# Index scores of a sparse-attention branch: plain float32 products replaced by one-pass products of split operands

## The chip, the cores and the metric

The kernel runs on one core of a Trainium2 chip. The metric is the time of one execution on the device in microseconds; the median of several runs is used. The core's engines work side by side, each with its own instruction queue: TensorE (matrix products; PE in the profile, with its weight loads as PEld), VectorE (DVE), ScalarE (ACT), GpSimd (POOL) and the DMA queues, most of which SyncE (SP) feeds.

## The reference

The model is a trunk of two layers on 256 tokens with 2048 channels. Each layer normalises its input, multiplies it by one large matrix and splits the result among three token mixers: a sparse attention, a convolution and a stick-breaking attention. Their gated outputs are merged and projected, and added to the input. The change touches the indexer of the sparse attention, which chooses for every query the 64 keys that it may attend to:

```python
qi = apply_rope(qi.reshape(b, s, IDX_HEADS, IDX_DIM), cos, sin)      # 16 heads of 128
ki = apply_rope(ki.reshape(b, s, 1, IDX_DIM), cos, sin)[:, :, 0]     # one key head
wi = wi * (IDX_HEADS ** -0.5) * (IDX_DIM ** -0.5)
...
for start in range(0, s, BLOCK_Q):                                   # blocks of 128 queries
    end = start + BLOCK_Q
    rel = jnp.einsum('bthd,bsd->bhts', qi[:, start:end], ki[:, :end])
    score = jnp.einsum('bhts,bth->bts', jax.nn.relu(rel), wi[:, start:end])
    score = jnp.where(causal[None], score, NEG_INF)
    _, idx = lax.top_k(score, min(top_k, end))                       # top_k = 64
    valid = idx <= tq[None, :, None]
    ...
```

So a score is a sum over 16 heads of a weight times the positive part of a product of a query and a key. The first 64 queries have at most 64 keys before them, so all of these are chosen and no score is needed.

## The kernel before

All large products go through `unit` (its parts in lines 238 to 277) and `mult` (line 280). A unit is 512 KB of a weight matrix: SyncE loads it into one of six buffers `raw` (line 253), ScalarE casts it to a rounded type, the high part `wh` (line 264), and VectorE subtracts that from the original, which leaves the low part `wl` (line 269). `wh` and `wl` have three buffers each. The activations are kept in high and low parts too, and a float32 product becomes three one-pass products: high by high, high by low and low by high. They add up in PSUM. A plain float32 product, without parts, is one call that TensorE runs as several passes.

`chunk_W`, `chunk_N` and `chunk_T` run over the units of one stretch of columns. `chunk_T` leaves the result transposed, channels on partitions. At the end of each unit `background` lets one waiting piece of smaller work put its instructions in: the steps of a `turn_in` (a transposition by DMA, lines 172 to 188) or of one of the first two `stages`, which are generators that say after how many units they want to go on. VectorE, ScalarE and the queues follow an order that is laid out by a scheduler from program order, with `high_priority` for casts, subtractions and the evacuation of results.

Around the change a layer runs in this order. The four stick-breaking stages are started; then come the chunks for the index key (`O_KI`), values and index weights, keys, and attention queries (`O_QA`, two chunks, each turned in and rotated by `spin`, lines 794 to 798, some time later). `finish` ends the stages. Then 8 chunks give the index queries, two heads each, for the tokens from 64 on (192 of 256). Each is evacuated by `summed` (lines 305 and 306) into a small buffer `ev` (three of them) and rotated by `rope` (lines 404 to 409), which writes into the tile `qiT`. The first 64 tokens of `qiT` are filled with zeros by GpSimd. A flag holds the convolution's work back during these chunks.

After that, `index(0)` and `index(1)` are started as stages and run beside the chunks of the merge gates. For each block of 128 queries, four groups of four heads are multiplied in plain float32 (line 820), ScalarE takes the positive part (line 823), and VectorE adds each head, times its weight, to the scores (line 826). Then VectorE chooses: eight rounds of the eight largest (line 831) and their replacement (line 832), and a mask from what was replaced (lines 833 and 834).

Of the kernel before, what the change touches and what calls it, by code (L numbers as in the profile page):

```python
# [54 lines left out]
def trunk(ctx: ExitStack, tc: tile.TileContext, x, xt, w_in, w_a, w_b, w_c, w_out,  # L55
# [37 lines left out]
    def nm(s):  # L93
        uid[0] += 1
        return f"{s}_{uid[0]}"
# [4 lines left out]
    def big():  # L100
        return [slot(), slot()]

    def at(b, k):
        return b[k // KC][:, k % KC, :]
# [92 lines left out]
    def start(gen):  # L197
        stages.append([gen, 0])
# [197 lines left out]
    def pair(n):  # L396
        return tuple(tp.tile([P, n], F32R, tag=t, bufs=2, name=nm(t)) for t in ("ph", "pl"))

    def rope(acc, dst):
        a, a3 = summed(acc)  # L400
        nh, nt = a3.shape[1:]
        sw = ev()[:, :nh * nt]
        with tc.high_priority():
            nc.scalar.copy(sw[0:64, :], a[64:128, :])
            nc.scalar.copy(sw[64:128, :], a[0:64, :])
            s3 = sw.rearrange("p (h t) -> p h t", h=nh)
            nc.vector.tensor_mul(dst, a3, cos2[:, :nh, S - nt:])
            nc.vector.tensor_mul(s3, s3, sin2[:, :nh, S - nt:])
            nc.vector.tensor_add(dst, dst, s3)

    def sigmoid_of(a):
        sg = ev()
        with tc.high_priority():
            nc.scalar.activation(sg, a, AF.Sigmoid)
        return sg.rearrange("p (h t) -> p h t", h=2)

    def gate(c0, o, b, w, hx, park=None, slots=True, turn=TURN):
        def gated(k, z, v):
# [71 lines left out]
    for layer in range(DEPTH):  # L490
# [281 lines left out]
            start(stick(h0))  # L772

        hold[0] = True
        kk_ = t4()
        kaT = kk_[:, :2 * S].rearrange("p (c t) -> p c t", c=2)
        kiT = kk_[:, 2 * S:3 * S].rearrange("p (c t) -> p c t", c=1)
# [5 lines left out]
        for t in range(NT):  # L783
            with tc.high_priority():
                split(va[0][:, t, :], va[1][:, t, :], a[t][:, :256])
                nc.scalar.mul(wi[:, t, :], a[t][:, 256:256 + NIH], WI_SCALE)
        rope(chunk_T(w, O_KA, 256, hx, KD), kaT)

        qaT = slot()
# [8 lines left out]
                nc.vector.tensor_add(a3, a3, s3)  # L798
# [12 lines left out]
        def index(t, qiT=qiT, kiT=kiT, wi=wi, bias=bias):  # L811
            n = (t + 1) * P
            cb = cst[:, C_CB + S - n:C_CB + S]
            sc = tp.tile([P, S], F32, tag="sc", bufs=2, name=nm("sc"))
            bs = tp.tile([P, S], F32, tag="bias", bufs=2, name=nm("bias"))
            for g in range(NIH // 4):
                ps = mm_tile()
                for q in range(4):
                    hd = g * 4 + q
                    nc.tensor.matmul(ps[:, q * n:(q + 1) * n], at(qiT, hd)[:, t * P:(t + 1) * P],  # L820
                                     kiT[:, 0, :n], start=True, stop=True)
                rl = t4()
                nc.scalar.activation(rl[:, :4 * n], ps[:, :4 * n], AF.Relu)
                for q in range(4):
                    hd = g * 4 + q
                    nc.vector.scalar_tensor_tensor(sc[:, :n], rl[:, q * n:(q + 1) * n], wi[:, t, hd:hd + 1],
                                                   cb if hd == 0 else sc[:, :n], op0=ALU.mult, op1=ALU.add)
                yield 2
            for _ in range(TOPK // 8):
                m8 = small(8)  # L830
                nc.vector.max(m8, sc[:, :n])
                nc.vector.match_replace(sc[:, :n], m8, sc[:, :n], TAKEN)
            nc.vector.tensor_scalar(bs[:, :n], sc[:, :n], -2e38, NEG, op0=ALU.is_gt, op1=ALU.mult)
            nc.vector.tensor_tensor(bs[:, :n], bs[:, :n], cb, op=ALU.min)
            bias[t] = bs
# [417 lines left out]
```

## Time and profile before

| what | value |
| --- | --- |
| median of 3 runs | 2019.34 us (2019.0 to 2019.47) |
| span of the profiled execution | 2016.9 us |
| TensorE busy | 2005.8 us, 9550 matmuls |
| VectorE busy | 1577.9 us |
| ScalarE busy | 1388.3 us |
| GpSimd busy | 104.8 us |
| bytes moved by DMA | 458.66 MB, mean 227 GB/s |
| granted TensorE clock | 0.999 |
| plain index products, first block (64 records) | 8.4 us busy |
| plain index products, second block (64 records) | 15.1 us busy |
| query chunks of layer one | 312.5 to 386.8 us |

The span goes from the first to the last instruction of one profiled execution; the median counts some 2.4 us around it. Busy time counts an engine as busy from the start of an instruction to its end, and matmuls overlap, so their durations are longer than the distance of their starts. An arrow such as "<-DVE wl L269" names what ended a wait: here VectorE's write of `wl` in line 269.

### The profile page before, as it was taken

The numbers are of one execution on the slowest core, as the hardware profiler recorded it, in microseconds if no ns is written. First come the engines' busy times: TensorE is split into PE (matmuls) and PEld (weight loads), VectorE is DVE, ScalarE is ACT, GpSimd is POOL, SyncE is SP. The second block draws the span as 40 slices with busy tenths as digits, with TensorE's granted clock in tenths as the row PEclk, the third lists the DMA queues.
The fourth block names the chain that finished last, engine by engine and source line by source line (L and its number), as shares of the span: only waits on it lengthen the run. The fifth ranks groups of instructions, "written<-read, shape, count | busy, mean of one in ns | idle before, by whom it ended". The sixth has DMA issues, their size and how long they took to land.

```text
span 2016.9 us, 26722 instructions
## 1 busy us (share of the span) xinstructions
PE 2005.8 (99%) x9550; PEld 1699.3 (84%) x9550; DVE 1577.9 (78%) x1750; ACT 1388.3 (69%) x1952; POOL 104.8 (5%) x160
## 2 busy tenths in 40 slices
PE   9999999999999999999999999999999999999998
PEld 7888889988888888888888888899888888888887
DVE  8688767897798888866676887678967988788665
ACT  7899666687776555556658986676877765555653
POOL 0000000000001200110000000000000012002100
PEclk9999999999999999999999999999999999999999
DMA  8787666656988877889867775676678789768983
GB/s 285 215 227 213 179 178 204 214 178 195 253 237 261 272 245 236 262 267 263 267 198 216 217 211 175 177 205 209 188 206 255 227 261 302 219 230 273 283 268 126
DMA packets 340278, 458.66 MB, mean 227 GB/s; under 512 B 109104, under 2 KB 159024, under 8 KB 340016
## 3 DMA queue, kind: packets, MB, share of 16 engines
q1 hardware_dynamic: 327040, 420.88, 69.7%
q0 software_dynamic: 11648, 33.56, 5.1%
q10 hardware_dynamic: 1456, 2.51, 0.4%
q8 instruction: 75, 1.23, 0.2%
q14 instruction: 59, 0.48, 0.1%
HBM read 413.37 MB, written 20.97 MB: 215 GB/s over the span
## 4 chain that ended last, share of the span: by engine, by line
PE 98%; DMA 1%; DVE 0%; ACT 0%; issue 0%; ACTq 0%; SPq 0%; DVEq 0%
PE acc L280 87%; PE mm L280 8%; PE mm L820 1%; PE mm L857 1%; PE mm L895 0%; PE mm L764 0%; PE mm L728 0%; DMA s<-s 0%; DMA raw<-in_w_in_dram 0%; DVE wl L269 0%; PE mm L750 0%; PE mm L731 0%; PE mm L766 0%; PE mm L755 0%; PE mm L752 0%
## 5 line engine op out<-in xcount | busy, mean ns | idle before, releaser
L280 PE MATMUL acc<-wh,s 128*128 128x512 f32 (+2 forms) x4736 | 1157.0, 386 | 1.2 <-ACT wh L264 1.1
L269 DVE TENSOR_TENSOR wl<-raw,wh 128x1024 fp32r<-128x1024 f32 (+2 forms) x714 | 857.2, 1207 | 294.8 <-ACT wh L264 277.0
L280 PEld LDWEIGHTS acc<-wh,s 128*128 128x128 f32 x4736 | 875.6, 188 | 177.4 <-ACT wh L264 1.5
L264 ACT CAST wh<-raw 128x1024 fp32r<-128x1024 f32 (+2 forms) x713 | 738.8, 1039 | 387.3 <-PE acc L280 304.5
L280 PE MATMUL acc<-wl,s 128*128 128x512 f32 (+2 forms) x2368 | 622.6, 385 | 0.0
L280 PEld LDWEIGHTS acc<-wl,s 128*128 128x128 f32 x2368 | 439.5, 188 | 89.1 <-DVE wl L269 0.2
L442 ACT ACTIVATE t<-s,cst 128x255 f32<-128x255 f32 (+14 forms) x480 | 199.9, 487 | 0.0
L445 DVE TENSOR_TENSOR s<-s,t 128x1020 f32<-128x1020 f32 (+14 forms) x120 | 138.4, 1153 | 0.0
L280 PE MATMUL acc<-s,wh 128*128 128x384 f32 (+1 forms) x608 | 125.8, 348 | 0.0
L280 PE MATMUL mm<-wh,s 128*128 128x512 f32 x448 | 119.7, 389 | 0.0
L280 PEld LDWEIGHTS acc<-s,wh 128*128 128x128 f32 x608 | 104.2, 189 | 3.2
L280 PEld LDWEIGHTS mm<-wh,s 128*128 128x128 f32 x448 | 84.1, 188 | 17.4
L231 POOL COPY sm<-sm 128x3 f32<-128x3 f32 x64 | 52.6, 821 | 544.6 <-ACT sm L230 544.6
L280 PEld LDWEIGHTS acc<-s,wl 128*128 128x128 f32 x608 | 79.0, 191 | 1.9 <-DVE wl L269 0.9
L280 PE MATMUL acc<-s,wl 128*128 128x192 f32 (+1 forms) x608 | 79.5, 273 | 0.6 <-DVE wl L269 0.6
L264 ACT CAST wh<-s 128x1024 fp32r<-128x1024 f32 x32 | 33.6, 1049 | 66.1 <-DVE s L1046 58.6
L280 PE MATMUL mm<-wl,s 128*128 128x512 f32 x224 | 69.1, 390 | 0.0
L264 ACT CAST wh<-t 128x1024 fp32r<-128x1024 f32 x32 | 33.6, 1050 | 40.5 <-DVE t L1046 28.0
L269 DVE TENSOR_TENSOR wl<-s,wh 128x1024 fp32r<-128x1024 f32 x32 | 39.2, 1225 | 24.0 <-ACT wh L264 23.7
L280 PEld LDWEIGHTS mm<-wl,s 128*128 128x128 f32 x224 | 41.9, 188 | 9.0 <-DVE wl L269 0.4
L269 DVE TENSOR_TENSOR wl<-t,wh 128x1024 fp32r<-128x1024 f32 x32 | 39.1, 1222 | 9.9 <-ACT wh L264 7.1
L1046 DVE TENSOR_TENSOR t<-raw,raw 128x1024 f32<-128x1024 f32 x32 | 39.0, 1219 | 0.0
(220 smaller groups left out, 1260.6 us busy)
## 6 DMA issues: line engine op xcount, KB each, us to landing
raw<-in_w_in_dram SPq DMA_DIRECT2D x570, 512.0 KB, 4.4
raw<-in_w_out_dram SPq DMA_DIRECT2D x64, 512.0 KB, 5.1
raw<-in_w_b_dram SPq DMA_DIRECT2D x32, 512.0 KB, 5.1
raw<-in_w_c_dram SPq DMA_DIRECT2D x32, 512.0 KB, 5.2
raw<-in_w_a_dram SPq DMA_DIRECT2D x32, 512.0 KB, 5.3
parked<-s POOLq DMA_DIRECT2D x16, 512.0 KB, 4.7
t<-gates POOLq DMA_DIRECT2D x16, 512.0 KB, 7.0
s<-parked POOLq DMA_DIRECT2D x32, 256.0 KB, 5.7
```

Source lines behind the costliest of these rows:

```text
L231: seen = nc.gpsimd.tensor_copy(copy[:, :3], mark)
L264: highs[0] = nc.scalar.copy(u[1], u[0])
L269: sub = nc.vector.tensor_sub(u[2], u[0], u[1].bitcast(F32))
L280: newest[0] = nc.tensor.matmul(o, lhsT, rhs, start=start, stop=stop, skip_group_check=True)
L442: nc.scalar.activation(o[:, i, :S - d], yT[:, c, :S - d], AF.Copy, scale=wq)
L445: nc.vector.tensor_add(to, to, o[:, :, :S - d])
L820: nc.tensor.matmul(ps[:, q * n:(q + 1) * n], at(qiT, hd)[:, t * P:(t + 1) * P], kiT[:, 0, :n], start=True, stop=True)
L857: nc.tensor.matmul(ps[:, q * n:(q + 1) * n], qaT[:, c * 4 + q, ts_], kaT[:, c, :n], start=True, stop=True)
L1046: nc.vector.tensor_tensor(o, a_, b_, op=op)
```

## The change

The index products no longer run in plain float32. Keys and queries are split into high and low parts, as the large products have them, and each product becomes three one-pass products.

- `rope` may now work in place in its evacuation buffer and hands the result to a function `halves`, inside its high-priority block. For the key this is a `split` into the new tile `ki`; for the queries it is `query_parts`, which makes two splits for each pair of heads: one for tokens 64 to 127, one for tokens 128 to 255. A split is a copy on ScalarE (line 393) and a subtraction on VectorE (line 394).
- The zero fill of the first 64 tokens goes. The queries lie in three large slots in place of two. The second `turn_in` of the attention queries therefore uses two small buffers (`t4`) for its words, not a slot.
- `index(0)` becomes `index_near`. Only the tokens 64 to 127 of the first block are computed, so two heads together fill the 128 columns of one stationary operand: the even head's scores come out on partitions 0 to 63 and the odd head's on 64 to 127. A group holds four such pairs, and there are two groups. The weights are arranged the same way in `wp_`. At the end the even half is copied to the other partitions and added, and the choice runs on 64 partitions. The mask of the first 64 queries is the causal one.
- `index(1)` becomes `index_far`, with the same four groups of four heads as before and three products for each head.
- A helper that nobody called, `sigmoid_of`, is removed.

```diff
-    def rope(acc, dst):
+    def rope(acc, dst, halves=None):
         a, a3 = summed(acc)
         nh, nt = a3.shape[1:]
+        dst = a3 if dst is None else dst
...
             nc.vector.tensor_add(dst, dst, s3)
+            if halves is not None:
+                halves(dst)
...
-        rope(chunk_T(w, O_KI, P, hx, KD), kiT)
+        kaT = t4()[:, :2 * S].rearrange("p (c t) -> p c t", c=2)
+        ki = tp.tile([P, 2 * S], F32R, tag="ki", bufs=1, name=nm("ki")).rearrange("p (i c t) -> p i c t", i=2, c=1)
+        rope(chunk_T(w, O_KI, P, hx, KD), None, partial(split, ki[:, 0], ki[:, 1]))
...
+        wp_ = small(NIH // 2 + 1, 2)[:, :NIH // 2]
+        wf = wi[:, 0, :].rearrange("p (g q) -> p g q", q=2)
+        nc.scalar.copy(wp_[0:64], wf[64:128, :, 0])
+        nc.scalar.copy(wp_[64:128], wf[64:128, :, 1])
...
-            turn_in(chunk_W(w, O_QA + h * P, hx), qaT[:, h:h + 4, :], partial(spin, qaT[:, h:h + 4, :]))
+            turn_in(chunk_W(w, O_QA + h * P, hx), qaT[:, h:h + 4, :], partial(spin, qaT[:, h:h + 4, :]), slots=h == 0)
         finish()
-        qiT = big()
-        for b in qiT:
-            nc.gpsimd.memset(b[:, :, :TOPK], 0.0)
+        qa2 = slot(F32R).rearrange("p a b -> p (a b)").rearrange("p (i h t) -> p i h t", i=2, h=NIH)
+        qb2 = [slot(F32R).rearrange("p a b -> p (a b)").rearrange("p (h t) -> p h t", h=NIH) for _ in range(2)]
+
+        def query_parts(h, v):
+            split(qa2[:, 0, h:h + 2, :], qa2[:, 1, h:h + 2, :], v[:, :, :TOPK])
+            split(qb2[0][:, h:h + 2, :], qb2[1][:, h:h + 2, :], v[:, :, TOPK:])
+
         for h in range(0, NIH, 2):
-            rope(chunk_T(w, O_QI + h * P, 256, hx, KD, TOPK), qiT[h // KC][:, h % KC:h % KC + 2, TOPK:])
+            rope(chunk_T(w, O_QI + h * P, 256, hx, KD, TOPK), None, partial(query_parts, h))
...
+        three = ((0, 0), (0, 1), (1, 0))
+
+        def index_near(qa2=qa2, ki=ki, wp_=wp_, bias=bias):
...
+            nc.vector.tensor_copy(sc[:, :P], cb)
+            nc.vector.memset(sc[:TOPK, :P], 0.0)
+            for g in range(2):
+                ps = mm_tile()
+                for q in range(4):
+                    h = g * 8 + q * 2
+                    for n, (i, j) in enumerate(three):
+                        nc.tensor.matmul(ps[:, q * P:(q + 1) * P], qa2[:, i, h:h + 2, :], ki[:, j, 0, :P],
+                                         start=n == 0, stop=n == 2)
...
+                yield 2
+            near, even = sc[TOPK:, :P], sc[TOPK:, P:]
+            nc.scalar.copy(even, sc[:TOPK, :P])
+            nc.vector.tensor_add(near, near, even)
+            nc.vector.tensor_copy(bs[:TOPK, :P], cb[:TOPK])
+            chosen(near, bs[TOPK:, :P], cb[TOPK:])
...
+        def index_far(qb2=qb2, ki=ki, wi=wi, bias=bias):
...
-                    nc.tensor.matmul(ps[:, q * n:(q + 1) * n], at(qiT, hd)[:, t * P:(t + 1) * P],
-                                     kiT[:, 0, :n], start=True, stop=True)
+                    for n, (i, j) in enumerate(three):
+                        nc.tensor.matmul(ps[:, q * S:(q + 1) * S], qb2[i][:, g * 4 + q, :], ki[:, j, 0, :],
+                                         start=n == 0, stop=n == 2)
...
-        for t in range(NT):
-            start(index(t))
+        start(index_near())
+        start(index_far())
```

`chosen` holds the rounds of choice and the mask, as they stood at the end of `index`.

More of the change, by code (lines that the diff above doesn't have):

```diff
@@ L409, in rope @@
             nc.vector.tensor_add(dst, dst, s3)
[L411 to L415, printed above, removed]
+            if halves is not None:
+                halves(dst)
     def gate(c0, o, b, w, hx, park=None, slots=True, turn=TURN):
@@ L806, in trunk, with chosen @@
+        def query_parts(h, v):
+            split(qa2[:, 0, h:h + 2, :], qa2[:, 1, h:h + 2, :], v[:, :, :TOPK])
+            split(qb2[0][:, h:h + 2, :], qb2[1][:, h:h + 2, :], v[:, :, TOPK:])
         for h in range(0, NIH, 2):
-            rope(chunk_T(w, O_QI + h * P, 256, hx, KD, TOPK), qiT[h // KC][:, h % KC:h % KC + 2, TOPK:])
+            rope(chunk_T(w, O_QI + h * P, 256, hx, KD, TOPK), None, partial(query_parts, h))
         hold[0] = False
         bias = {}
-        def index(t, qiT=qiT, kiT=kiT, wi=wi, bias=bias):
-            n = (t + 1) * P
-            cb = cst[:, C_CB + S - n:C_CB + S]
+        def chosen(sc, bs, cb):
+            for _ in range(TOPK // 8):
+                m8 = small(8)[-sc.shape[0]:]
+                nc.vector.max(m8, sc)
+                nc.vector.match_replace(sc, m8, sc, TAKEN)
+            nc.vector.tensor_scalar(bs, sc, -2e38, NEG, op0=ALU.is_gt, op1=ALU.mult)
+            nc.vector.tensor_tensor(bs, bs, cb, op=ALU.min)
@@ new lines, in trunk @@
+        three = ((0, 0), (0, 1), (1, 0))
+        def index_near(qa2=qa2, ki=ki, wp_=wp_, bias=bias):
+            cb = cst[:, C_CB + P:C_CB + S]
+            sc = tp.tile([P, S], F32, tag="sc", bufs=2, name=nm("sc"))
+            bs = tp.tile([P, S], F32, tag="bias", bufs=2, name=nm("bias"))
+            nc.vector.tensor_copy(sc[:, :P], cb)
[7 more added lines that the diff above has]
+                                         start=n == 0, stop=n == 2)
+                rl = t4()
+                nc.scalar.activation(rl[:, :4 * P], ps[:, :4 * P], AF.Relu)
+                for q in range(4):
+                    nc.vector.scalar_tensor_tensor(sc[:, :P], rl[:, q * P:(q + 1) * P],
+                                                   wp_[:, g * 4 + q:g * 4 + q + 1], sc[:, :P],
+                                                   op0=ALU.mult, op1=ALU.add)
+                yield 2
[4 more added lines that the diff above has]
+            chosen(near, bs[TOPK:, :P], cb[TOPK:])
+            bias[0] = bs
@@ L814, in index @@
+        def index_far(qb2=qb2, ki=ki, wi=wi, bias=bias):
+            cb = cst[:, C_CB:C_CB + S]
             sc = tp.tile([P, S], F32, tag="sc", bufs=2, name=nm("sc"))
@@ L818, in index @@
                 for q in range(4):
-                    hd = g * 4 + q
-                    nc.tensor.matmul(ps[:, q * n:(q + 1) * n], at(qiT, hd)[:, t * P:(t + 1) * P],
-                                     kiT[:, 0, :n], start=True, stop=True)
+                    for n, (i, j) in enumerate(three):
+                        nc.tensor.matmul(ps[:, q * S:(q + 1) * S], qb2[i][:, g * 4 + q, :], ki[:, j, 0, :],
+                                         start=n == 0, stop=n == 2)
                 rl = t4()
-                nc.scalar.activation(rl[:, :4 * n], ps[:, :4 * n], AF.Relu)
+                nc.scalar.activation(rl, ps, AF.Relu)
                 for q in range(4):
                     hd = g * 4 + q
-                    nc.vector.scalar_tensor_tensor(sc[:, :n], rl[:, q * n:(q + 1) * n], wi[:, t, hd:hd + 1],
-                                                   cb if hd == 0 else sc[:, :n], op0=ALU.mult, op1=ALU.add)
+                    nc.vector.scalar_tensor_tensor(sc, rl[:, q * S:(q + 1) * S], wi[:, 1, hd:hd + 1],
+                                                   cb if hd == 0 else sc, op0=ALU.mult, op1=ALU.add)
                 yield 2
[L829 to L835, printed above, removed]
-        for t in range(NT):
-            start(index(t))
+            chosen(sc, bs, cb)
+            bias[1] = bs
+        start(index_near())
+        start(index_far())
         def early(b, j):
```

3 lines of the change are left out of this document (removed).

## The prediction

> **What bounds the kernel now.** The first view is the page: span, busy times, and the chain that ended last.
>
> ```profile
> span 2016.9 us, 26722 instructions
> ...
> PE 2005.8 (99%) x9550; PEld 1699.3 (84%) x9550; DVE 1577.9 (78%) x1750; ACT 1388.3 (69%) x1952; POOL 104.8 (5%) x160
> ...
> PE 98%; DMA 1%; DVE 0%; ACT 0%; issue 0%; ACTq 0%; SPq 0%; DVEq 0%
> PE acc L280 87%; PE mm L280 8%; PE mm L820 1%; PE mm L857 1%; PE mm L895 0%; PE mm L764 0%; PE mm L728 0%; DMA s<-s 0%; DMA raw<-in_w_in_dram 0%; DVE wl L269 0%; PE mm L750 0%; PE mm L731 0%; PE mm L766 0%; PE mm L755 0%; PE mm L752 0%
> ```
>
> TensorE is busy for 2005.8 of 2016.9 us, and the chain runs through it for 98% of the span, nearly all in the products of line 280. Nothing else ends last for any length of time. So a microsecond taken out of TensorE's work is worth a microsecond of time, and a microsecond taken out of another engine is worth nothing; but work added to another engine costs as soon as it makes a product wait. Both have to be counted.
>
> The second view is the list of TensorE's instructions by line and shape, for the index scores (line 820) that the change rewrites.
>
> ```profile
> L820 PE MATMUL mm<-t,s 128*128 128x256 f32 x64 | 15.1, 378 | 0.0
> ...
> L820 PE MATMUL mm<-t,s 128*128 128x128 f32 x64 | 8.4, 274 | 0.0
> ```
>
> 64 records of each shape are 2 layers x 16 heads x 2: each plain float32 call shows as two records. The mean durations overlap their neighbours, so they are no price. The price comes from starts, in the timeline of TensorE at the index stage:
>
> ```profile
> 389.60 1.05 PE L820 MATMUL mm<-t,s 128*128 128x128 f32 x8
> ...
> 393.22 1.89 PE L820 MATMUL mm<-t,s 128*128 128x256 f32 x8
> ...
> 397.68 1.05 PE L820 MATMUL mm<-t,s 128*128 128x128 f32 x8
> ...
> 421.94 1.98 PE L280 MATMUL acc<-wh,s 128*128 128x512 f32 x8
> ...
> 424.66 1.98 PE L280 MATMUL acc<-wh,s 128*128 128x512 f32 x8
> ```
>
> Between index groups lies one unit of the gate product (8 + 4 matmuls); a unit alone takes 424.66 - 421.94 = 2.72 us. So a group of the first block costs 393.22 - 389.60 - 2.72 = **0.90 us** for 8 records (0.1125 each) and one of the second block 397.68 - 393.22 - 2.72 = **1.74 us** (0.2175 each). Four of each make 10.56 us a layer. As a check, the four rounds from 389.60 to 421.94 are 32.34 us, less 8 x 2.72 leaves 10.58.
>
> **The change part by part: the products.** The second block's 16 heads become 48 one-pass products of 256 columns. Their price is in this timeline, four one-pass products of 256 columns in the scores of the stick-breaking branch:
>
> ```profile
> 303.01 0.28 PE L752 MATMUL mm<-ph,ones_r 128*128 128x256 f32 x1
> ...
> 303.48 2.02 PE L280 MATMUL acc<-wh,s 128*128 128x512 f32 x8
> ```
>
> (303.48 - 303.01) / 4 = 0.1175 us. So 48 x 0.1175 = 5.64 us in place of 4 x 1.74 = 6.96: **1.32 us less** a layer.
>
> The first block's 16 heads become 8 pairs of 3 products of 128 columns, 24 in all. No one-pass product of 128 columns is in the trace. The nearest is the one of 192 columns:
>
> ```profile
> 346.97 1.03 PE L280 MATMUL acc<-s,wl 128*128 128x192 f32 x8
> 347.83 1.59 PE L280 MATMUL acc<-s,wh 128*128 128x384 f32 x8
> ```
>
> 8 take 347.83 - 346.97 = 0.86 us, 0.108 each. If time followed columns alone, from 0.1175 at 256 columns, 192 would take 0.088 and 128 would take 0.059. It took 0.108, and the two-pass record that streams 128 columns twice took 0.1125 with its own load of 128 stationary columns. So below some 256 columns something other than the stream sets the pace. Bounds for one product are 0.059 and 0.1125; I take 0.11, as the 192-column row lies at that end. 24 x 0.11 = 2.64 us in place of 4 x 0.90 = 3.60: **0.96 us less** a layer (2.18 at the other end). Together 2.28 us a layer, **4.5 us** for both: this term is on the path in full.
>
> The Trainium skill, "TensorE: Matmul & The Clock Gate", section "Back-to-back issue gap", gives about 81 ns per matmul of 128 columns in a stream of loads and products. No run here shows it; by it the first block would gain 0.70 us more a layer (estimate). This is the second rival.
>
> The same page of the Trainium skill, section "The mechanism", says that a load of weights overlaps running matmuls only where the row groups differ. Here all rows are used, so by it a product would pay load and stream one after the other and the change would lose on TensorE. By it the new products would cost 24 x (0.11 + 0.059) + 48 x (0.11 + 0.1175) = 15.0 us a layer, 4.4 more than now (estimate). The trace decides against it: TensorE's 9550 matmuls stand beside 9550 loads in the first rows above, one each, and yet the 256-column products follow each other in 0.1175 us. It gets no chance of its own.
>
> **What is added around the products.** Each of the 8 query chunks a layer (two heads, 192 tokens each) now ends with two splits: two copies on ScalarE and two subtractions on VectorE, of 128 and 256 elements. Their VectorE price is from start to start: 256 elements from an existing split, 128 from the nearest shape.
>
> ```profile
> 250.52 0.42 DVE L394 TENSOR_TENSOR t<-acc,t 128x256 fp32r<-128x256 f32 x1
> 250.86 0.95 DVE L394 TENSOR_TENSOR pl<-t,ph 128x768 fp32r<-128x768 f32 x1
> ```
>
> ```profile
> 433.98 0.28 DVE L834 TENSOR_TENSOR bias<-bias,cst 128x128 f32<-128x128 f32 x1
> 434.17 1.23 DVE L269 TENSOR_TENSOR wl<-raw,wh 128x1024 fp32r<-128x1024 f32 x1
> ```
>
> 0.34 + 0.19 = **0.53 us** a chunk by starts, 0.70 by durations (0.42 + 0.28). I use 0.6. ScalarE's two copies lie below the row of 384 elements:
>
> ```profile
> L404 ACT COPY ev<-ev 64x384 f32<-64x384 f32 x16 | 8.2, 512 | 11.6 <-DVE ev L306 11.3
> L305 ACT COPY ev<-acc 128x384 f32<-128x384 f32 x16 | 7.5, 472 | 0.0
> ```
>
> at most 2 x 0.47 = 0.94 us, nearer 0.55. What hides this? The stage of the query chunks, in the view of busy time by stretch (columns: PE, PEld, VectorE, ScalarE, GpSimd):
>
> ```profile
> 312.50:386.80 74.30, 73.69 (x515) 73.38 (x514) 60.34 (x74) 50.55 (x66) 0.00 (x0) 1.00 0.72 220
> ```
>
> VectorE has 60.3 of 74.3 us; 8 x 0.6 fits on average, and ScalarE has 24 us free. In most chunks the cover is VectorE's own waiting, as here:
>
> ```profile
> 350.58 1.22 DVE L269 TENSOR_TENSOR wl<-raw,wh 128x1024 fp32r<-128x1024 f32 x1 [1.06 <-ACT wh L264]
> ...
> 353.90 0.56 DVE L408 TENSOR_TENSOR ev<-ev,cst 128x384 f32<-128x384 f32 x1 [1.03 <-ACT ev L405]
> ```
>
> But the cover fails where the rotation of the attention queries (lines 794 to 798) is put between the chunks. VectorE, first layer:
>
> ```profile
> 327.22 0.56 DVE L409 TENSOR_TENSOR s<-s,ev 128x384 f32<-128x384 f32 x1
> 327.69 1.22 DVE L269 TENSOR_TENSOR wl<-raw,wh 128x1024 fp32r<-128x1024 f32 x1
> 328.83 0.68 DVE L796 TENSOR_TENSOR s<-s,cst 128x512 f32<-128x512 f32 x1
> ...
> 331.84 1.21 DVE L269 TENSOR_TENSOR wl<-raw,wh 128x1024 fp32r<-128x1024 f32 x1
> 332.98 0.68 DVE L798 TENSOR_TENSOR s<-s,ev 128x512 f32<-128x512 f32 x1
> ```
>
> TensorE at the same place:
>
> ```profile
> 330.91 1.59 PE L280 MATMUL acc<-s,wh 128*128 128x384 f32 x8
> 333.11 1.14 PE L280 MATMUL acc<-s,wl 128*128 128x192 f32 x8 [0.60 <-DVE wl L269]
> ```
>
> The weights' low half that started at 331.84 was late, and TensorE stood still for 0.60 us. Here VectorE has no slack: the subtractions of the chunk whose rotation ended at 327.22 come, at the earliest, behind the product's low half of 327.69, and push the one at 331.84 back. The stall grows by 0.6. The second pass of the rotation, and the first in the second layer:
>
> ```profile
> 359.11 1.22 DVE L269 TENSOR_TENSOR wl<-raw,wh 128x1024 fp32r<-128x1024 f32 x1
> 360.25 0.68 DVE L798 TENSOR_TENSOR s<-s,ev 128x512 f32<-128x512 f32 x1
> ```
>
> ```profile
> 360.73 1.03 PE L280 MATMUL acc<-s,wl 128*128 128x192 f32 x8
> ```
>
> ```profile
> 1331.55 1.22 DVE L269 TENSOR_TENSOR wl<-raw,wh 128x1024 fp32r<-128x1024 f32 x1
> 1332.69 0.68 DVE L798 TENSOR_TENSOR s<-s,ev 128x512 f32<-128x512 f32 x1
> ```
>
> ```profile
> 1333.01 1.03 PE L280 MATMUL acc<-s,wl 128*128 128x192 f32 x8
> ```
>
> The low half is free by the next start (360.25 and 1332.69), and its product starts at 360.73 and 1333.01: slack of 0.48 and 0.32 us. 0.6 costs 0.12 and 0.28 there. The second pass of layer two I take like that of layer one, 0.12. Sum: **+1.1 us** (0.6 + 0.12 + 0.28 + 0.12). Bounds: -0.6, if the order changes so that today's stall goes; above, see the third rival.
>
> **What costs nothing.** The key's split (256 elements, once a layer) and two tiny copies of the weights lie in a stage where TensorE has no stall; bounds 0 to 0.4 us. In the index stage VectorE loses 8 of 16 score updates of the first block, by this row 8 x 0.35 = 2.8 us,
>
> ```profile
> L826 DVE SCALAR_TENSOR_TENSOR sc<-t,sm,sc 128x128 f32<-128x128 f32 x30 | 10.5, 349 | 0.6
> ```
>
> and gains a copy, a fill and an addition, under 1 us; selection on 64 partitions handles the same 128 columns, so I take its time as unchanged. None of it was on the path. The fill of the query tiles on GpSimd goes, and nobody waited for it. Each rotated chunk now stays in its evacuation buffer (three of them) until its subtractions are done, some 1.5 us longer; the attention rotation waits behind that on ScalarE, and the casts behind it; I take 0, as one of the other two buffers is free, with up to 1.5 us per pass as the bound. The second turn of the attention queries moves from a large slot to two small buffers. Its transposes wait today for the last stick-breaking copy, which frees a slot:
>
> ```profile
> SPq L178 <- ACT s L768: 1.1, 1, 1.1
> ```
>
> The loads behind them on the same queue wait too. ScalarE's own copies of that turn come first and last 2 us, so I expect no gain; bounds -1.1 and +1.1.
>
> **Sum.** Span 2016.9 - 4.5 + 1.1 = 2013.5 us. The median of the runs is 2019.34, 2.4 above this span; with the same difference kept, **2015.9 us**.
>
> **Rivals.** The first: the splits are fully hidden, because the order puts them behind the late low halves or breaks up the rotation. Then 2019.3 - 4.5 = 2014.8, or 2014.2 if today's 0.60 us stall goes too. For it: the 14 us that VectorE has free. Against: the rows at 327 to 333.
>
> The second: products of 128 columns keep a pace near 0.08 us: 24 x 0.03 x 2 = 1.4 us better, 2014.5. Against: 0.108 at 192 columns.
>
> The third ends on the other side: the splits turn into a chain between ScalarE and VectorE, and the kernel is slower. Each subtraction waits for a copy on the other engine. With one such wait of 1.03 us (row at 353.90) the delay per chunk is 0.53 + 1.03 = 1.6 us. The four passes of the rotation then cost 1.6 + 1.12 + 1.28 + 1.12 = 5.1 us, which gives 2019.3 - 4.5 + 5.1 = 2019.9; if the chunk behind each pass is late too, about as much again, near 2024. It decides from a delay of 1.45 us per chunk, where 4 x 1.45 less the slacks of 1.28 eats the 4.5 us. Against it: VectorE can take a ready low half between the two.
>
> The fourth, half of it: the first block gains nothing (each of its products at 0.15), or the splits go ahead of the low halves in every chunk and cost twice as much. 2019.3 - 2.6 + 1.1 = 2017.8, or 2019.3 - 4.5 + 2.3 = 2017.1; up to 2019.
>
> **How the numbers follow.** Forecast (2015.0 to 2017.0): 0.42. First rival: 0.22. Second: 0.06. Third: 0.10. Fourth (2017 to 2019): 0.20. The range 2013.6 to 2020.4 leaves out the far part of the third and little of the second. A measurement of this kernel can tell about 0.2% from no change, which is 4.0 us, so faster means below 2015.3: most of the first and second rival and the low edge of the forecast, 0.35. Slower means above 2023.4, the far part of the third: 0.04. Within: 0.61.
>
> **What would show it.** In the changed kernel's timeline of TensorE, the first block's two groups should take 12 x 0.11 = 1.3 us each and the second block's four 1.4 us each, beside units of 2.72. Stalls "<-DVE wl L269" should stand in the query chunks where the attention rotation runs, four of them, 1.1 us above today's 0.6 in sum. No stall at all there makes the first rival right; stalls over 5 us, with VectorE waiting for ScalarE at the splits, the third. A first-block product well off 0.11 us breaks the first term.

## The result

| what | before | after |
| --- | --- | --- |
| median of 4 runs each, side by side | 2019.17 us (2018.93 to 2019.47) | 2034.88 us (2033.16 to 2036.18) |
| ratio after to before | | 1.0078, 95% interval 1.0063 to 1.0092 |
| span of the profiled execution | 2016.9 us | 2031.4 us |

The kernel became slower by 15.7 us, where 3.4 us less were forecast and the range ended at 2020.4. Of the four executions of the kernel after, the two with a granted clock of 0.999 took 2033.16 (the profiled one) and 2033.75 us, and those with 0.997 and 0.998 took 2036.01 and 2036.18. The page of the kernel after:

```profile
span 2031.4 us, 26822 instructions
...
PE 2007.4 (99%) x9566; PEld 1695.1 (83%) x9566; DVE 1586.4 (78%) x1776; ACT 1394.7 (69%) x1988; POOL 103.0 (5%) x156
```

TensorE is busy only 1.6 us longer than before (2005.8), while the span grew by 14.5: the time went into standing still, not into products. To find the places, each product of line 280 (there are 9088 in both kernels, in the same order) was taken by its start in the one trace and in the other. How much the difference of the two starts grows over a stage is what the stage lost. The same was done for every experiment below; the numbers are microseconds against the kernel before, layer one / layer two. A rise in the start-up, which no edit explains, is in the last column and differs by up to 1.2 us between profiled executions. Not in the table, and not followed further, are 0.3 us between the layers in E2, E4, E6 and E9, and about 0.9 us near the end in E2 and E3.

| kernel | query chunks | index groups | choice and attention | start-up |
| --- | --- | --- | --- | --- |
| after | +5.2 / +6.1 | -2.0 / -2.0 | +3.4 / +3.3 | +0.4 |
| E1 before, fill late | +1.6 / +2.5 | 0 / 0 | 0 / 0 | +0.3 |
| E2 after, early fill | +3.0 / +4.0 | -2.0 / -2.0 | +3.3 / +4.3 | +0.6 |
| E3 after, choice on 128 partitions | +5.2 / +6.1 | -2.0 / -2.0 | 0 / 0 | +0.6 |
| E4 both | +3.0 / +4.1 | -2.0 / -2.0 | 0 / 0 | +0.9 |
| E5 E4, not in place | +1.3 / +2.4 | -2.0 / -2.0 | 0 / 0 | +0.1 |
| E6 E4, splits on GpSimd | +2.5 / +3.4 | -2.0 / -2.0 | 0 / 0 | +0.2 |
| E7 E5 and E6 | +3.7 / +5.2 | -2.0 / -2.0 | 0 / 0 | +0.3 |
| E8 pairs in plain float32 | +1.0 / 0 | -1.8 / -1.8 | 0 / 0 | +1.1 |
| E9 E8 without fill | +1.9 / +2.7 | -1.8 / -1.8 | 0 / 0 | +0.6 |
| E10 E8, choice on 64 partitions | +0.3 / 0 | -1.8 / -1.8 | +0.8 / +1.1 | +1.3 |
| E11 E8, far block split | +1.4 / +0.9 | -2.9 / -2.9 | 0 / 0 | +0.8 |

**The index groups gained, as forecast.** TensorE's timeline of the kernel after:

```profile
395.19 1.45 PE L836 MATMUL mm<-ki,s 128*128 128x128 f32 x12
...
399.30 1.58 PE L860 MATMUL mm<-ki,s 128*128 128x256 f32 x12
...
403.47 1.45 PE L836 MATMUL mm<-ki,s 128*128 128x128 f32 x12
```

With the unit of 2.72 us between them, a group of pairs takes 399.30 - 395.19 - 2.72 = 1.39 us for 12 products (0.116 each), and a group of the second block 403.47 - 399.30 - 2.72 = 1.45 us (0.121 each). A layer has two of the first and four of the second, 8.6 us in place of 10.6.

**The query chunks lost.** TensorE's timeline of the kernel after, first layer, where the attention queries are rotated and one rotation later:

```profile
337.20 1.14 PE L280 MATMUL acc<-s,wl 128*128 128x192 f32 x8 [1.44 <-DVE wl L269]
...
343.40 1.14 PE L280 MATMUL acc<-s,wl 128*128 128x192 f32 x8 [1.18 <-DVE wl L269]
...
365.36 1.14 PE L280 MATMUL acc<-s,wl 128*128 128x192 f32 x8 [0.66 <-DVE wl L269]
```

Before, there was one stall of 0.60 us here. Two reasons can be read in VectorE's timeline of the kernel after:

```profile
325.91 0.56 DVE L408 TENSOR_TENSOR ev<-ev,cst 128x384 f32<-128x384 f32 x1 [1.66 <-ACT ev L406]
...
329.56 0.77 DVE L186 COPY s<-s 128x1024 uint16<-128x1024 uint16 x1
330.21 0.74 DVE L186 COPY s<-t 128x1024 uint16<-128x1024 uint16 x1
330.85 1.21 DVE L269 TENSOR_TENSOR wl<-raw,wh 128x1024 fp32r<-128x1024 f32 x1
332.97 0.69 DVE L796 TENSOR_TENSOR s<-s,cst 128x512 f32<-128x512 f32 x1 [0.92 <-ACT ev L795]
...
335.93 1.22 DVE L269 TENSOR_TENSOR wl<-raw,wh 128x1024 fp32r<-128x1024 f32 x1
```

One is the two copies of line 186, 0.65 us each by starts. They turn the attention queries' words. In the kernel before, VectorE made them in idle time, when each had waited (the number in brackets):

```profile
312.78 0.78 DVE L186 COPY s<-s 128x1024 uint16<-128x1024 uint16 x1 [0.76 <-PE mm L766]
...
319.26 0.78 DVE L186 COPY s<-s 128x1024 uint16<-128x1024 uint16 x1 [2.29 <-DMA s<-s]
```

Now they stand in the rotation, and so do ScalarE's, in the timeline of ScalarE of the kernel after:

```profile
329.09 1.38 ACT L188 COPY s<-s 128x1024 uint16<-128x1024 uint16 x1
330.32 1.35 ACT L188 COPY s<-t 128x1024 uint16<-128x1024 uint16 x1
331.69 0.62 ACT L794 COPY ev<-s 64x512 f32<-64x512 f32 x1
```

The rotation's own copy (line 794) comes only behind them. The other reason is the wait of 1.66 us ahead of line 408, the first multiplication of the index queries' rotation, for ScalarE's half copies.

**A new stall stands behind the index groups**, in both layers. TensorE's timeline of the kernel after:

```profile
435.37 1.20 PE L280 MATMUL acc<-wl,s 128*128 128x512 f32 x4 [2.42 <-DVE wl L269]
```

In layer two the same product, at 1442.71, waits 2.40 us. VectorE at the same time as the first, in the kernel after: the choice of the first block (lines 818 to 821, on the 64 partitions from 64 to 127), mixed with score updates of the second (line 866).

```profile
427.55 1.22 DVE L269 TENSOR_TENSOR wl<-raw,wh 128x1024 fp32r<-128x1024 f32 x1
...
430.30 0.09 DVE L819 MATCH_VALUE_LOAD sc<-sm,sc 64x8 f32 x1
430.40 0.28 DVE L819 MATCH_REPLACE8 sc<-sm,sc 64x128 f32<-64x128 f32 x1
430.71 0.49 DVE L866 SCALAR_TENSOR_TENSOR sc<-t,sm,sc 128x256 f32<-128x256 f32 x1
431.23 0.29 DVE L818 MAX8 sm<-sc 64x8 f32<-64x128 f32 x1
431.55 0.48 DVE L866 SCALAR_TENSOR_TENSOR sc<-t,sm,sc 128x256 f32<-128x256 f32 x1
432.07 0.09 DVE L819 MATCH_VALUE_LOAD sc<-sm,sc 64x8 f32 x1
...
434.09 1.23 DVE L269 TENSOR_TENSOR wl<-raw,wh 128x1024 fp32r<-128x1024 f32 x1
```

From the subtraction of 427.55 to the next one at 434.09 VectorE makes no low half, and the product of 435.37 waits for it.

### The profile page after: what moved, and what is told of

It reads as the page before. It is cut to its first block, busy times and chain, and to the rows that moved or that the text cites. A ratio compares the mean times of both kernels' runs of the same rounds, so it can differ in the third digit from the quotient of the medians.

```text
span 2031.4 us, 26822 instructions
## 1 busy us (share of the span) xinstructions
PE 2007.4 (99%) x9566; PEld 1695.1 (83%) x9566; DVE 1586.4 (78%) x1776; ACT 1394.7 (69%) x1988; POOL 103.0 (5%) x156
## 3 DMA queue, kind: packets, MB, share of 16 engines
q8 instruction: 75, 1.23, 0.3%
## 5 line engine op out<-in xcount | busy, mean ns | idle before, releaser
L881 POOL DMA_DIRECT2D gates<-t x8 | 6.0, 745 | 1120.6 <-ACT t L880 1120.6
```

Source lines behind the costliest of these rows:

```text
L881: nc.gpsimd.dma_start(gates[b][:, :, j * 512:(j + 1) * 512].rearrange("t p d -> p t d"), sg_)
```

## The experiments

The kernel before, run beside the experiments, had medians of 2019.15 to 2019.27 us.

### E1 to E4: the fill and the 64 partitions

E1 is the kernel before, with GpSimd's zero fill moved behind each chunk's rotation:

```diff
-        for b in qiT:
-            nc.gpsimd.memset(b[:, :, :TOPK], 0.0)
...
+            nc.gpsimd.memset(qiT[h // KC][:, h % KC:h % KC + 2, :TOPK], 0.0)
```

> The kernel before, with one edit: the zero fill of the first 64 tokens of each query chunk is done behind that chunk's rotation and not ahead of all chunks. No split, no other product. In the instruction order this puts both turn copies of the attention queries (lines 186 and 188) behind the first query chunk's evacuation, right ahead of the rotation of the attention queries, as they stand in the changed kernel; before, they stand some four units earlier. Theory 1 (the displaced copies make the low halves late): stalls of 1 to 3 us a layer in the query chunks, 2 to 6 us slower than before, 2021 to 2025. Theory 2 (the splits alone make them late): within 0.7 us of before, 2019.

E2 is the kernel after, with a fill of 64 columns in each of the three query tiles ahead of the chunks:

```diff
+        for v in (qa2, qb2[0], qb2[1]):
+            nc.gpsimd.memset(v.rearrange("p i h t -> p (i h t)")[:, :TOPK].bitcast(F32) if v is qa2
+                             else v.rearrange("p h t -> p (h t)")[:, :TOPK].bitcast(F32), 0.0)
         def query_parts(h, v):
```

> The changed kernel, with a zero fill of the first 64 columns of each of its three query slots by GpSimd ahead of the chunks; the values are overwritten. It puts the turn copies back to where they stand in the kernel before. Theory 1 (displaced copies): the loss in the query chunks falls from 11 us in both layers to 2 to 5, and the median to 2026 to 2029. Theory 2 (splits): the loss stays, 2033 to 2036.

E3 is the kernel after, with the choice on all 128 partitions, the first 64 of which are overwritten by the causal mask afterwards:

```diff
+            chosen(sc[:, :P], bs[:, :P], cb)
             nc.vector.tensor_copy(bs[:TOPK, :P], cb[:TOPK])
-            chosen(near, bs[TOPK:, :P], cb[TOPK:])
```

> The changed kernel with the choice for the first block on all 128 partitions (the rows of the first 64 queries are chosen too, then overwritten by the causal mask); VectorE's order is the same up to the end of the choice. Theory A (instructions on 64 partitions do not overlap their neighbours, and that makes the low half late): the spacing of the eight rounds shrinks by about 0.1 us an instruction, the stall of 2.4 us a layer at the choice falls below 1.2, and the median by 2.4 to 5 us to 2030 to 2032.5. Theory B (only the order is at fault: the first block's choice now lies between the second block's score updates): the stall stays at 2.0 to 2.6 us and the median within 1 us of the changed kernel.

E4 has the edits of E2 and E3.

> Both edits of the two runs before it. If the two losses are separate, the gains add: with theories 1 and A 2022 to 2026; with theory 1 alone 2026 to 2029; with theory A alone 2030 to 2033.

| run | median us | ratio to before, 95% interval |
| --- | --- | --- |
| E1 | 2023.05 | 1.0019 (1.0010 to 1.0029) |
| E2 | 2030.97 | 1.0058 (1.0042 to 1.0075) |
| E3 | 2027.10 | 1.0039 (1.0024 to 1.0054) |
| E4 | 2023.14 | 1.0019 (1.0009 to 1.0028) |

E1 changes nothing but the place of a fill that no engine waited for, and costs 3.8 us. TensorE's and VectorE's timelines of E1:

```profile
333.25 1.14 PE L280 MATMUL acc<-s,wl 128*128 128x192 f32 x8 [0.46 <-DVE wl L269]
...
336.92 1.14 PE L280 MATMUL acc<-s,wl 128*128 128x192 f32 x8 [1.11 <-DVE wl L269]
```

```profile
324.16 0.56 DVE L407 TENSOR_TENSOR s<-ev,cst 128x384 f32<-128x384 f32 x1
324.64 1.41 DVE L186 COPY s<-s 128x1024 uint16<-128x1024 uint16 x2
...
330.77 0.69 DVE L796 TENSOR_TENSOR s<-s,cst 128x512 f32<-128x512 f32 x1 [2.57 <-ACT ev L795]
```

Both copies of line 186 now follow the first multiplication of the first chunk, and the rotation starts late, after waiting 2.57 us for ScalarE, which has the copies of line 188 to make as well. So a write into the query tiles early in program order is enough to have the scheduler place the copies of the attention queries early. E2 shows the same from the other side: with such a write they are back at their old place (313.37 and 319.89 in VectorE's timeline) and 3.9 us go. Why the scheduler does so was not followed further.

E3 takes 7.8 us away by doing twice as many rows. In the table the whole loss behind the index groups and in the attention stage goes with it, 6.7 us; the rest of the 7.8 was not traced to a place. VectorE's timeline of E3, with the same instructions as above:

```profile
425.01 1.22 DVE L269 TENSOR_TENSOR wl<-raw,wh 128x1024 fp32r<-128x1024 f32 x1
...
427.39 0.08 DVE L819 MATCH_VALUE_LOAD sc<-sm,sc 128x8 f32 x1
427.46 0.28 DVE L819 MATCH_REPLACE8 sc<-sm,sc 128x128 f32<-128x128 f32 x1
427.65 0.48 DVE L866 SCALAR_TENSOR_TENSOR sc<-t,sm,sc 128x256 f32<-128x256 f32 x1
428.04 0.29 DVE L818 MAX8 sm<-sc 128x8 f32<-128x128 f32 x1
428.25 0.47 DVE L866 SCALAR_TENSOR_TENSOR sc<-t,sm,sc 128x256 f32<-128x256 f32 x1
428.63 0.09 DVE L819 MATCH_VALUE_LOAD sc<-sm,sc 128x8 f32 x1
...
430.02 1.22 DVE L269 TENSOR_TENSOR wl<-raw,wh 128x1024 fp32r<-128x1024 f32 x1
431.16 0.22 DVE L849 COPY bias<-cst 64x128 f32<-64x128 f32 x1
431.29 0.41 DVE L818 MAX8 sm<-sc 128x8 f32<-128x256 f32 x1
```

On 128 partitions an instruction starts before the end of the one ahead of it: 428.25 + 0.47 = 428.72, and the next starts at 428.63. In the rows of the kernel after, with the choice on partitions 64 to 127, none does: 431.55 + 0.48 = 432.03, and the next starts at 432.07.

The number of partitions alone isn't the reason. The copy of line 849, in the last rows of E3, has 64 partitions too and overlaps both its neighbours: it starts at 431.16, ahead of 430.02 + 1.22 = 431.24, and the next starts at 431.29, ahead of 431.16 + 0.22 = 431.38. It lies on partitions 0 to 63, so it starts on the same partition as its neighbours on all 128. And in E10 (below), where the replacement's two instructions follow a maximum that is on partitions 64 to 127 as well, they overlap: 426.68 + 0.09 = 426.77, and the second starts at 426.75. So the rows fit a hold where work that starts at partition 64 alternates with work that starts at partition 0. This is argued from the rows; no run put the choice on partitions 0 to 63.

The same eleven instructions, from the load of line 819 (430.30 and 427.39) to the next subtraction, take 434.09 - 430.30 = 3.79 us there and 430.02 - 427.39 = 2.63 us here.

E4 shows that the two add up (3.9 + 7.8 = 11.7 us, 2034.88 to 2023.14). With a gain of 4.0 us in the index groups it is still 3.9 us slower than the kernel before: the query chunks lose 7.1 us, and the start-up of its profile another 0.9.

### E5 to E7: what the splits cost

Theory A says that the rotation in place is what costs, theory B that it is the work of the splits. The list of waits of E4 between 312 and 392 us (engine, line, what was waited for: us in total, times, longest) has the pattern of A:

```profile
ACT s L393 <- DVE ev L410: 8.9, 7, 1.6
DVE ev L408 <- ACT ev L406: 7.7, 7, 1.1
```

The multiplication of line 408 writes into the buffer that ScalarE is still copying from. In the kernel before it wrote into the query tile, in line 407 without waiting, while ScalarE copied. E5 is E4 with a separate buffer for the result:

```diff
-        dst = a3 if dst is None else dst
+        dst = (tp.tile([P, 1024], F32, tag="ph", bufs=2, name=nm("ph"))[:, :nh * nt]
+               .rearrange("p (h t) -> p h t", h=nh) if dst is None else dst)
```

> The kernel after, with the early fill back, the choice on 128 partitions, and one more edit: the rotation of keys and queries writes its result into a separate buffer, so its first multiplication on VectorE no longer waits until ScalarE has read the evacuation buffer. All of the computation is there. It starts from the run with the first two edits (2023.14 us, 3.9 above the kernel before), which loses 3.0 us in the query stage of layer one and 3.9 in that of layer two against the kernel before. Theory A (the in-place write makes VectorE wait for ScalarE in every chunk, and that delays the low halves of the weights): the waits of the multiplication for ScalarE's half copies (7.7 us in seven waits in layer one) go, at least 4 of the 6.9 us go, about 2018.5. Theory B (VectorE's two additional subtractions a chunk, some 0.65 us, are what is late; the wait only takes idle time): within 1 us of 2023. A result between, near 2021, makes it both.

E6 is E4 with the splits of the queries on GpSimd, E7 has both edits:

```diff
-            split(qa2[:, 0, h:h + 2, :], qa2[:, 1, h:h + 2, :], v[:, :, :TOPK])
-            split(qb2[0][:, h:h + 2, :], qb2[1][:, h:h + 2, :], v[:, :, TOPK:])
+            for hh, ll, src in ((qa2[:, 0, h:h + 2, :], qa2[:, 1, h:h + 2, :], v[:, :, :TOPK]),
+                                (qb2[0][:, h:h + 2, :], qb2[1][:, h:h + 2, :], v[:, :, TOPK:])):
+                nc.gpsimd.tensor_copy(hh, src)
+                nc.gpsimd.tensor_sub(ll, src, hh.bitcast(F32))
```

> The kernel after, with the early fill back, the choice on 128 partitions, and the copies and subtractions of the query splits put on GpSimd, which is idle in this stage; the rotation still works in place. All of the computation is there. Theory A (the in-place wait is what costs): VectorE still waits for ScalarE's half copies in every chunk, 7.7 us in layer one, so at most a third of the 6.9 us goes: 2021 to 2023. Theory B (the added work on VectorE and ScalarE costs): nearly all of it goes, since both engines then do in this stage what they did before: 2016 to 2018. A third possibility: GpSimd is so slow at the splits that the evacuation buffers come free late; then ScalarE's evacuations wait for it and the time rises above 2025.

> Both edits of the two runs before together: the rotation into a separate buffer and the query splits on GpSimd, on top of the early fill and the choice on 128 partitions. All of the computation is there. VectorE and ScalarE then have in the query stage the work of the kernel before. Theories A and B agree here: the 6.9 us of the query stages go whole, and what stays are the products, 3.8 to 4.0 us less than the kernel before: about 2015.4. If it stays above 2018, something else than A and B (GpSimd's hold on the buffers, or an order that differs) is late in the query stage.

| run | median us | ratio to before, 95% interval |
| --- | --- | --- |
| E5 | 2019.01 | 0.9999 (0.9990 to 1.0008) |
| E6 | 2021.79 | 1.0013 (1.0004 to 1.0022) |
| E7 | 2022.73 | 1.0018 (1.0009 to 1.0026) |

E5 takes 4.1 us away, 3.4 of them in the query chunks. The waits of E5 in the same stretch:

```profile
ACT s L393 <- DVE ph L410: 6.1, 5, 1.2
DVE ev L409 <- ACT ev L406: 4.6, 7, 1.0
```

No multiplication of line 408 waits any more; line 409 still waits, as its input is the copied half. A is right for about half: 3.7 of the 7.1 us stay in the query chunks, and B was to account for these. E6 gave 1.3 us back and not nearly all, as A expected. E7 had to come out near 2015.4 by both, and missed it by 7 us. The rows point to GpSimd, in two ways. First, it is slow, and VectorE is slower beside it. One of GpSimd's four groups of E6 in this stage, and VectorE's timeline of E6:

```profile
L812 POOL CAST s<-ev 128x256 fp32r<-128x256 f32 x7 | 8.6, 1231 | 0.0
```

```profile
331.58 0.95 DVE L796 TENSOR_TENSOR s<-s,cst 128x512 f32<-128x512 f32 x1
332.45 1.75 DVE L269 TENSOR_TENSOR wl<-raw,wh 128x1024 fp32r<-128x1024 f32 x1
```

A copy of 256 elements takes 1.23 us on GpSimd, and while it worked (until 333.13) the multiplication of line 796 took 0.95 us in place of 0.68 and the low half 1.75 in place of 1.22. The Trainium skill, "GPSIMD Engine Reference", section "8. Key points", states that GpSimd and VectorE contend where VectorE has two SBUF inputs; these rows agree, as all of these instructions have two.

Second, E7's stall grew to 1.79 us, and TensorE was slow behind it. TensorE's timeline of E7, and its busy time by stretch (columns: PE, PEld, VectorE, ScalarE, GpSimd, granted clock, DMA share, GB/s):

```profile
334.71 1.46 PE L280 MATMUL acc<-s,wl 128*128 128x192 f32 x8 [1.79 <-DVE wl L269]
335.96 2.81 PE L280 MATMUL acc<-s,wh 128*128 128x384 f32 x8
```

```profile
334.70:338.60 3.90, 3.89 (x17) 3.89 (x18) 3.85 (x5) 1.61 (x3) 0.00 (x0) 0.58 0.65 169
```

Eight products of 384 columns took 2.81 us in place of 1.59, and the clock was 0.58 for 3.9 us. It happened in layer two as well, behind a stall of 1.78 us. A clock that low costs about 0.42 x 3.9 = 1.6 us a layer (estimate), so it isn't all of the 7 us. So E7 doesn't measure what the splits cost without their work on VectorE, and B alone stays untested by it; E11 comes nearest.

### E8 to E11: pairs without splits

E8 asks what the pairing is worth alone. It is the kernel before with two heads on one stationary operand in plain float32; ScalarE copies the near queries of each chunk side by side into a small buffer `qn`. The fill stays, and the choice runs on 128 partitions.

```diff
             nc.vector.tensor_add(dst, dst, s3)
+            if near is not None:
+                nc.scalar.copy(near, dst[:, :, :TOPK])
...
+                    nc.tensor.matmul(ps[:, q * P:(q + 1) * P], qn[:, g * 8 + h:g * 8 + h + 2, :], kiT[:, 0, :P],
+                                     start=True, stop=True)
```

> The kernel before with one part of the change alone: two heads share one stationary operand in the first block, in plain float32, without any split. ScalarE copies the near queries side by side into a small buffer in each chunk; the zero fill stays and the choice runs on 128 partitions. The second block is as before. All of the computation is there. The first block then has 8 plain products of 128 columns a layer in place of 16, so 16 records in place of 32 at 0.1125 us: 1.8 us less a layer, 3.6 in all. If the losses come from the splits and the displaced work alone, the query stages stay within 0.5 us of the kernel before and the time is about 2015.6 (ratio 0.9982). If a copy of 0.3 us a chunk on ScalarE is enough to make the rotation late, some of the 3.6 us is lost again, 2017 to 2018.

E9 is E8 without the fill:

```diff
-        for v in qiT:
-            nc.gpsimd.memset(v[:, :, :TOPK], 0.0)
```

> The pairs in plain float32 of the run before (2016.07 us, span 2015.5), without the zero fill of GpSimd in the first 64 tokens of the query tiles. Nothing reads these tokens any more, so all of the computation is there, and there are no splits of queries or keys. Theory C (the fill's only worth is the place of the attention queries' copies: without it the scheduler puts both of VectorE's copies into the rotation of the first query chunk): the stalls of the query stage grow as they did in the kernel before with the fill made late, by about 2 us a layer, so 2019 to 2021. Rival: the copies are late only together with the splits; then the time stays within 1 us of 2016.

E10 is E8 with the choice on 64 partitions:

```diff
-            chosen(sc[:, :P], bs[:, :P], cb)
             nc.vector.tensor_copy(bs[:TOPK, :P], cb[:TOPK])
+            chosen(near, bs[TOPK:, :P], cb[TOPK:])
```

> The pairs in plain float32 (2016.07 us, span 2015.5) with the fill, and the choice of the first block on 64 partitions as in the kernel after. All of the computation is there. Theory D (instructions of 64 partitions do not overlap their neighbours on VectorE, so the choice of both blocks holds the low half of the weights back): a stall of about 2.5 us a layer behind the index groups, and up to 0.9 us a layer more in the attention stage: 2020 to 2023. Rival: the choice is late only because the splits delay the scores; then there is no such stall and the time is within 1 us of 2016.

E11 is E8 with the second block's products split; the rotation works into a separate buffer, as in E5.

```diff
+            nc.scalar.copy(qn[:, h:h + 2, :], v[:, :, :TOPK])
+            split(qb2[0][:, h:h + 2, :], qb2[1][:, h:h + 2, :], v[:, :, TOPK:])
...
-                    nc.tensor.matmul(ps[:, q * S:(q + 1) * S], at(qiT, g * 4 + q)[:, P:], kiT[:, 0, :],
-                                     start=True, stop=True)
+                    for n, (i, j) in enumerate(three):
+                        nc.tensor.matmul(ps[:, q * S:(q + 1) * S], qb2[i][:, g * 4 + q, :], ki[:, j, 0, :],
+                                         start=n == 0, stop=n == 2)
```

> The pairs in plain float32 for the first block, and split, one-pass products for the second block alone; rotation into a separate buffer, fill and choice on 128 partitions as before. All of the computation is there. The index stage then gains 1.80 us a layer in the first block (16 records fewer at 0.1125) and 4 x 0.29 = 1.16 in the second, 5.9 us in all. Each query chunk has one split of 256 elements in place of two. If that split costs as much in the query stage as half of what was lost with the result in a separate buffer (1.8 us in layer one, 2.6 in layer two), the loss is 2.2 us in all: about 2015.6, 0.5 below the pairs alone. If it costs the whole 4.4 us, as what counts is that there is a split in the rotation's place: about 2017.8, 1.7 above the pairs alone. So it tells whether one-pass products are worth their splits at all, in the block where they gain.

| run | median us | ratio to before, 95% interval |
| --- | --- | --- |
| E8 | 2016.07 | 0.9984 (0.9975 to 0.9993) |
| E9 | 2020.45 | 1.0006 (0.9997 to 1.0015) |
| E10 | 2017.94 | 0.9995 (0.9986 to 1.0004) |
| E11 | 2015.86 | 0.9983 (0.9974 to 0.9992) |

E8 beats both kernels, by 3.2 us and 18.8 us, and lies near the 2015.6 expected. TensorE's timeline of E8:

```profile
391.74 1.05 PE L836 MATMUL mm<-t,t 128*128 128x128 f32 x8
...
395.38 1.89 PE L859 MATMUL mm<-t,s 128*128 128x256 f32 x8
```

A group of eight heads takes 395.38 - 391.74 - 2.72 = 0.92 us for 8 records, against 1.39 us for the 12 one-pass products of the same heads. So in the first block the pairing makes all of the gain, and the split takes some of it back.

E9 confirms the fill: nothing reads what it writes, and without it the time rises by 4.4 us, with no split in the kernel. TensorE's timeline of E9 has the stalls of E1's kind:

```profile
333.74 1.14 PE L280 MATMUL acc<-s,wl 128*128 128x192 f32 x8 [0.64 <-DVE wl L269]
...
337.41 1.14 PE L280 MATMUL acc<-s,wl 128*128 128x192 f32 x8 [0.57 <-DVE wl L269]
```

E10 lies between what its theory and the rival expected. It is 1.9 us slower than E8, and the table puts all of that in the choice and attention stage, but the 2.5 us of stall behind the index groups didn't come. The stalls are one of 0.34 us behind ScalarE and this one, in TensorE's timeline of E10:

```profile
1442.32 1.20 PE L280 MATMUL acc<-wl,s 128*128 128x512 f32 x4 [0.73 <-DVE wl L269]
```

Neither stands beside the choice on partitions 64 to 127: between the two subtractions ahead of this one (1437.14 and 1441.05) VectorE has only instructions on 128 partitions. So E10 shows that this choice costs time without splits too, but not by which wait. The 2.4 us of the kernel after need the order as well: there, two rounds of the choice and four score updates stand between two subtractions (rows at 430.30 to 434.09), while in VectorE's timeline of E10 the score updates end at 426.31 and subtractions stand at 427.06, 429.51 and 433.07. Why the order differs was not tried.

E11 expected 2015.6 if one split of 256 elements costs half of what two cost in E5, and 2017.8 if it costs all. It is at 2015.86, near half: its query chunks lose 2.3 us, E5's 3.7. Against E8 the second block gains 2.9 - 1.8 = 1.1 us a layer by its split, 2.2 in both. The query chunks lose 1.3 us more than E8's in the table, but E8's trace has a stall of 0.70 us at 323.72, behind ScalarE's cast, that E10's, with the same work in its query chunks, has not. Against E10's 0.3 us they lose 2.0 more, so 0.2 us of the gain is left. The medians leave 0.2 us too, and the intervals of E8 and E11 don't tell them apart.

## Why the prediction was wrong

By its own steps, in the order of the size of the error:

- **"selection on 64 partitions handles the same 128 columns, so I take its time as unchanged. ... None of it was on the path."** Failed, 6.7 us (3.4 and 3.3 in the table); E3 takes this away. The time of one instruction is indeed unchanged (0.28 to 0.29 us for 128 columns in both), but the distance to the next is not, and the choice came to stand beside the second block's score updates, where 6.5 us pass without a low half (427.55 to 434.09). The step priced durations and looked only at the sum of VectorE's work, which fell; it didn't ask what would stand between two subtractions.
- **"The fill of the query tiles on GpSimd goes, and nobody waited for it."** The sentence is true and the price of nothing was wrong: 4.2 us (11.3 in the query chunks of the kernel after, 7.1 in E4). E1 and E9 show it in two kernels that have no split. Not a wait but the scheduler's order hung on it.
- **The rotation in place** was not priced. The prediction gave a bound of 1.5 us per pass for the buffer that is held longer and took 0; the wait of line 408 for ScalarE, 7.7 us in E4's layer one, was not seen. By E5 it costs 3.4 us (7.1 less 3.7).
- **The splits, +1.1 us.** Mis-sized: 3.7 us stay in E5, where the other causes are gone. That these are all the splits' is not shown by a run without them; with one split a chunk in place of two, E11 loses 2.0 us more in the query chunks than E10, which has none. The four stalls of the forecast were not the matter: where the rotation begins, E5 has one of 0.74 us in layer one (1.2 forecast, 0.6 of it from before) and one of 0.69 in layer two (0.28 forecast). The rest is delays of 0.1 to 0.4 us at other products of the chunks, where the sum let the splits hide.
- **The products, -4.5 us.** Right in kind, and 4.0 in size: 0.116 us a product in place of 0.11, and 0.121 in place of 0.1175. The second rival, with 0.08 us a product of 128 columns, is out; the Trainium skill's "TensorE: Matmul & The Clock Gate", section "Back-to-back issue gap", gives about 81 ns for it, and the trace shows 0.116 us in a stream with a load ahead of each product.

The third rival, slower through a chain between ScalarE and VectorE, came nearest: E4, which has only the splits and the rotation in place, is at 2023.14, and that rival gave 2019.9 to near 2024. Waits between the two engines are there (line 393 for line 410, 8.9 us in seven waits), but at the splits themselves (line 394 for line 393) VectorE waited 1.8 us in five waits only. The multiplication that waits for the half copies makes about half of E4's loss (3.4 of 7.1 us), and it wasn't named; so the rival was near in size by another wait than its own. Even without the fill and the choice, the time would have passed the range's upper end of 2020.4.

The sum of the parts, for the trace: start-up 0.4, fill 4.2, in place 3.4, splits 3.7, choice 6.7, products -4.0, which is 14.4 of the 14.5 us. The 15.7 us between the medians are 1.2 more, as the profiled executions are not the median ones. A run takes about 1.8 us more than its own span (2033.16 against 2031.4), so the 2.4 us between median and span of the kernel before hold some of that too.

## What to carry to other kernels

An instruction that nobody waits for can still be what fixes the order: before it is taken out of a kernel whose queues a scheduler lays out, list which instructions stand near it in program order and look for them in the new order of each engine. On an engine that feeds the bound one, price a changed stretch by the longest time between two of its deliveries, not by its sum. And where an instruction writes in place, look for the reader on the other engine that it must now wait for.

## What the hardware showed beside that

The choice on partitions 64 to 127 took VectorE longer than the one on all 128: 3.79 us in place of 2.63 for the same eleven instructions. Seven of them stand on the upper half, and in the rows shown each of the eleven starts only after the end of the one ahead, while a copy on partitions 0 to 63 overlaps its neighbours (E3, 431.16 to 431.29).

TensorE's clock fell to 0.58 for 3.9 us behind a stall of 1.79 us in E7, and stayed at 1.00 behind the 2.42 us of the kernel after. E2 has both in one execution: a stall of 2.63 us ahead of 433.54 in layer one, and one of 2.42 us ahead of 1438.73 in layer two. Its busy time by stretch (columns as above):

```profile
433.50:437.50 4.00, 3.96 (x17) 3.30 (x18) 4.00 (x11) 3.87 (x7) 0.00 (x0) 1.00 0.66 160
1438.70:1442.70 4.00, 3.97 (x10) 3.12 (x11) 3.93 (x9) 2.96 (x6) 0.00 (x0) 0.57 0.65 167
```

The longer stall left the clock at 1.00, the shorter one brought it to 0.57; E2's 4.3 us in layer two, against the 3.3 of the kernel after, go with that. So the length of the stall alone doesn't decide. The Trainium skill, "TensorE: Matmul & The Clock Gate", section "What's actually happening", says that the clock halves after an idle window of about 3.4 us, counted in windows that run on their own. E7 disagrees on the length, as its stall was half of that; that it depends on where in time the stall lies would fit E2's two stalls, but no run here tests it.
